# Scans in fewer TensorE batches, 64-row scores of both maps, another pace of the first and last head, and modulation dots held behind a norm

## The chip, the cores and the metric

The kernel runs on one core of a Trainium2 chip. A core has TensorE (matrix products, in the profile PE, its weight loads PEld), VectorE (DVE), ScalarE (ACT), GpSimd (POOL) and SyncE (SP, which here issues the loads and stores). Every engine works through its own queue in order and waits on semaphores that other engines raise. TensorE reads from the on-chip memory and writes into eight accumulator banks of 128 partitions x 512 fp32 values; VectorE and ScalarE read the results from there. The metric is device time of one execution in microseconds (us), as the median of several runs.

## The reference, cut to what matters

One inference step of two layers over 512 latent tokens and 128 context tokens, with width 1024. Layer 0 mixes tokens with a two-directional state-space scan (32 heads in 4 groups, chunks of 128 tokens), layer 1 with differential attention (8 heads, two key maps of width 64 each). Each is followed by a channel mixer. Every sub-layer is normed and modulated by shift, scale and gate, which are products of SiLU(cond) with a weight matrix.

```python
def modulation(cvec, w, b):
    m = jax.nn.silu(cvec) @ w + b
    return jnp.split(m[:, None, :], 6, axis=-1)

def ssd_scan(x, dt, a, bm, cm, h0):               # one direction
    ...
    decay = jnp.exp(jnp.where(tri, seg, -jnp.inf))
    cb = jnp.einsum('bcign,bcjgn->bcijg', cm, bm)
    y_diag = jnp.einsum('bcijge,bcjgep->bcigep', cb[..., None] * decay, xd)
    xw = xd * jnp.exp(a_cs[:, :, -1:] - a_cs)[..., None]
    states = jnp.einsum('bcqgn,bcqgep->bcgepn', bm, xw)
    ...                                            # h_in: states carried from chunk to chunk
    y_off = jnp.einsum('bcqgn,bcgepn->bcqgep', cm, h_in) * jnp.exp(a_cs)[..., None]
    y = (y_diag + y_off).reshape(b, l, nh, p)

def diff_attend(q, k, v, lam):                     # per block of 128 queries
    s = jnp.einsum('bqhcd,bkhcd->bhcqk', qi, k) * DA_SCALE    # c: the two maps
    p = jax.nn.softmax(s, axis=-1)
    w = p[:, :, 0] - lam * p[:, :, 1]
    return jnp.einsum('bhqk,bkhd->bqhd', w.astype(v.dtype), v)
```

Latent queries see 640 keys (512 latent, 128 cached context); context queries see the 128 context keys. The forward and backward scans of a chunk are summed, gated by SiLU(z) and normed by group.

## The kernel before, in words

**Layout.** Activations lie feature-major: 128 features on the partitions, 640 tokens in the free dimension (512 latent, then 128 context). A weight product gives one output tile of 128 features x 640 tokens. Weights arrive as fp32 through SP's queue (`prefetch`, three units ahead, four buffers `raw`) and are split into a high and a low part (`whi` by ScalarE, `wlo` by VectorE, lines 93 and 99 through helpers); activations are split in the same way. A tile is the sum over k of three products, high x high, low x high, high x low, each in two column pieces (256 and 384 columns), so eight k-steps of six matmuls for a width of 1024. All these matmuls are issued at line 102.

**Accumulators.** Three wide buffers of two banks each (`psd`, tag d) serve the weight products and some of the other work; two single banks (`psm`, tags m and y) serve the rest.

**Interleaving.** After each k-step `dense_many` calls `hook` (L74), which advances the generators in the task list; `yield n` asks to be called again n k-steps (ticks) later. So the scans, the attention heads, the norms and the modulation dots run in pieces between the k-steps of weight products. `drain` runs a task to its end at once. The order in the code is not yet the order on the engines: the framework plans each engine's queue ahead of time by its own estimates of durations, takes the earliest instruction in code order that it believes ready, and lets later ready work fill a hole. A tile's buffer must be free before its first writer is planned, so who holds a buffer also sets who can run early.

**Scan** (`ssd_group`, L668, one task per group, while the next tiles x, B, C and z are produced): B and x are transposed chunk by chunk (btp, xtp), the backward states are carried (st: `xw` on VectorE, then a product, then two VectorE steps), and then for every chunk: the product of C and B (cb); for each of two quartets of heads the logarithmic decays of both directions (r, bf16, 96 rows) which ScalarE and VectorE turn into the operands m and qc; four ticks later the quartet's outputs (yp: products of 64 stationary columns into the upper and the lower half of the partitions in turn), added to xf by VectorE; and the next forward state.

**Attention** (`attention`, L1028; `att_head`, L939; `att_tail`, L985): for every head the tiles q, k and v are produced; rotary positions and the split of q and k run on VectorE and ScalarE (`att_q`, `att_k`). For precision the score of a map is made of two products over 128 rows: q's 64 features lie twice, high part on its own half, low part on the other, and k's high part lies on both halves, its low part likewise:

```python
st[m][o] = hi(q); st[m][x] = lo(q)          # o: the map's half, x: the other half
kk = (kh[m] on both halves, kl[m] on both halves)
```

A score tile (sl) takes a wide buffer; VectorE takes the row maximum from it, ScalarE the exponent and the sum, and then it is free. Context scores (sp) are fp32 products over the 64 rows of a map. The tail transposes the weights of all four query blocks, multiplies with v and norms the head. The last head's tail runs under the output projection of the first six heads.

**Norm and modulation.** The weight products that end a sub-layer give the first 256 tokens (half A) and the rest (half B) separately; `norm_task` (L227) norms each half while the next sub-layer's first three tiles run on the other (`start_tiles`, L287). `rms_bcast` sums squares on TensorE (ms), takes the reciprocal root in nine short VectorE steps, and spreads it over the partitions (nbc). `mod_rest` (L478) makes layer 1's modulation on VectorE during ffn0: it loads the conditioning (`cbc`), applies SiLU, and takes 96 dot products (L500) with rows loaded into `mw`; in the code it begins 48 ticks into ffn0, and it is due before ffn0's last weight products.

Of the kernel before, what the change touches and what calls it, by code (L numbers as in the profile page):

```python
# [9 lines left out]
F32 = mybir.dt.float32  # L10
# [8 lines left out]
P = 128  # L19
D = 1024  # L20
# [25 lines left out]
class Step:  # L46


    def __init__(self, ctx, tc, a):
# [7 lines left out]
        self.modtask = None  # L57
        self.down = False
# [168 lines left out]
    def norm_task(self, half, gs, sh, h):  # L227
# [94 lines left out]
    def mod_slots(self, pool, odd, name):  # L322
# [5 lines left out]
        return [xt[:, i, :] for i in range(5)] + [t("qm", 2, i) for i in (5, 6)] + [t("qc0", 1, 7)]  # L328
# [339 lines left out]
    def ssd_group(self, g, xf, Bf, Cf, pool):  # L668

        nc = self.nc  # L670
# [8 lines left out]
        pm = self.psm.tile([P, 512], F32, tag="m", name="btp")  # L679
        for c in range(4):  # L680
            nc.tensor.transpose(pm[:, c * P:(c + 1) * P], Bf[:, c * P:(c + 1) * P], self.ident)
        self.act(bt[:, 0:4, :].rearrange("p c n -> p (c n)"), pm, AF.Copy)
        yield 1
        pm = self.psm.tile([P, 512], F32, tag="m", name="btp")
        nc.tensor.transpose(pm[:, :P], Bf[:, 4 * P:5 * P], self.ident)
        self.act(bt[:, 4, :], pm[:, :P], AF.Copy)
        yield 1
        for c in (3, 2, 1, 4, 0):
            pm = self.psm.tile([P, 512], F32, tag="m", name="xtp")
            for t in range(4):  # L690
                nc.tensor.transpose(pm[:, t * P:(t + 1) * P], xf[t][:, c * P:(c + 1) * P], self.ident)
            self.act(xt[:, c, :], pm, AF.Copy)
            yield 1

        def state(d_, c, out):

            hc = slice(32 * d_ + 8 * g, 32 * d_ + 8 * g + 8)
            xw = sl("xw", "xw", 512, 1)
            v3 = lambda t: t.rearrange("p (h e) -> p h e", h=8)
            self.tt(v3(xw), v3(xt[:, c, :]), self.wst[:, c, hc].unsqueeze(2).to_broadcast([P, 8, 64]), ALU.mult)  # L700
            pm = self.psm.tile([P, 512], F32, tag="m", name="st")
            self.mm(pm, bt[:, c, :], xw, True, True)
            nh = sl("hs", f"h_{d_}_{c}_", 512, 6)
# [4 lines left out]
            self.tt(v3(nh), v3(hs[d_, c]), self.cd[:, c, hc].unsqueeze(2).to_broadcast([P, 8, 64]), ALU.mult)  # L708
# [3 lines left out]
        for c in (3, 2, 1):  # L712
            state(1, c, c - 1)
            yield 2
        for d_ in range(2):
            state(d_, NL, None)
            yield 2

        b4 = lambda ap: ap.unsqueeze(1).to_broadcast([P, 4, P])
        v4 = lambda t: t.rearrange("p (h i) -> p h i", h=4)  # L720
        for c in range(NCH):
            cs = slice(c * P, (c + 1) * P)
            pm = self.psm.tile([P, 512], F32, tag="m", name="cb")
# [5 lines left out]
            for q in range(2):  # L729
                h0 = 8 * g + 4 * q  # L730
                r = self.psd.tile([P, 1024], F32, tag="d", name="r")
                for h in range(4):
                    for d_ in range(2):
                        self.mm(r[:, 512 * d_ + h * P:512 * d_ + (h + 1) * P],
                                self.oh[:, h0 + h:h0 + h + 1].to_broadcast([96, P]), self.R3[d_][:, cs], True, True)
                e = sl("qe", "e", 512, 2)
                m = sl("qm", "m", 512, 2)
                for h in range(4):
                    hh = slice(h * P, (h + 1) * P)
                    self.act(e[:, hh], r[:, hh], AF.Identity, bias=self.C[:, c, h0 + h:h0 + h + 1])  # L740
                    self.act(m[:, hh], r[:, 512 + h * P:512 + (h + 1) * P], AF.Identity,
                             bias=self.C[:, c, 32 + h0 + h:33 + h0 + h])
                self.tt(e, e, m, ALU.min)
                self.act(e, e, AF.Exp)
                for h in range(4):
                    hh = slice(h * P, (h + 1) * P)
                    self.act(m[:, hh], cbb, AF.Copy, scale=self.dt[:, c, 32 + h0 + h:33 + h0 + h])
                    self.stt(m[:, hh], cbf, self.dt[:, c, h0 + h:h0 + h + 1], m[:, hh], ALU.mult, ALU.add)
                self.tt(m, m, e, ALU.mult)
                cs2 = []  # L750
                if c < NL:
                    for d_ in range(2):
                        x = sl(f"qc{d_}", f"qc{d_}", 512, 1)
                        self.act(x, r[:, 512 * d_:512 * d_ + 512], AF.Exp)
                        self.tt(v4(x), v4(x), b4(Cf[:, cs]), ALU.mult)
                        cs2.append(x)
                yield 4
                yp = self.psm.tile([P, 512], F32, tag="y", name="yp")
                for pr in range(2):
                    nt = 1 + len(cs2)  # L760
                    for i in range(nt):
                        for hh in range(2):
# [4 lines left out]
                            self.mm(yp[64 * hh:64 * hh + 64, pr * P:(pr + 1) * P], lhsT, rhs, i == 0, i == nt - 1)  # L767
                for pr in range(2):
                    t = 2 * q + pr
                    self.stt(xf[t][:, cs], xf[t][:, cs], self.svec[:, 4 * g + t:4 * g + t + 1],  # L770
                             yp[:, pr * P:(pr + 1) * P], ALU.mult, ALU.add)
                yield 1
            if c < NL - 1:
                state(0, c, c + 1)
                yield 1
# [98 lines left out]
    def att_v(self, ps, hd, vs, pool):  # L874
# [11 lines left out]
        yield 1  # L886
# [28 lines left out]
    def att_q(self, x, hd, pool):  # L915
# [3 lines left out]
        st = [pool.tile([P, TS], F32R, tag=f"qs{m}", name=f"qs{m}_{hd}", bufs=2) for m in range(2)]  # L919
        for m, (o, x) in enumerate(((slice(0, 64), slice(64, 128)), (slice(64, 128), slice(0, 64)))):  # L920
            self.act(st[m][o], q[o], AF.Copy, scale=DA_SCALE)
            self.stt(st[m][x], q[o], DA_SCALE, st[m][o].bitcast(F32), ALU.mult, ALU.subtract)
        return st

    def att_k(self, x, hd, pool):
# [4 lines left out]
        hi, lo = ([pool.tile([P, T], F32R, tag=f"k{nm}{m}", name=f"k{nm}{m}_{hd}", bufs=1) for m in range(2)]  # L930
                  for nm in "hl")
        for m, (o, x) in enumerate(((slice(0, 64), slice(64, 128)), (slice(64, 128), slice(0, 64)))):
            self.act(hi[m][o], k[o], AF.Copy)
            self.tt(lo[m][o], k[o], hi[m][o].bitcast(F32), ALU.subtract)
            self.act(hi[m][x], hi[m][o].bitcast(F32), AF.Copy)
            self.nc.vector.tensor_copy(lo[m][x], lo[m][o].bitcast(F32))
        return hi, lo

    def att_head(self, hd, qp, kp, qs, k, vs, o, pool):  # L939

        nc = self.nc
# [287 lines left out]
```

## Time and profile before

| what | us |
|---|---|
| median of 3 runs | 1940.85 (1938.77 to 1942.29) |
| the profiled execution: its own time | 1941.6 |
| its span, first to last instruction | 1939.8 |
| TensorE busy in it | 1892.0 |
| VectorE busy in it | 1397.2 |
| ScalarE busy in it | 967.6 |

The span is covered by the stages in this order: first tiles and modulation to about 60 us, the scan layer with its output projection to 604, ffn0 to 1070, attention to 1456, ffn1 to the end. The granted TensorE clock over the span was 0.992.

A line of the timeline has the start and the length in us, the engine, the line, the operation, what it writes and reads, its form (for a matmul rows x stationary columns, then the moving operand), how many were put together, and in brackets the idle time of the engine before it with what ended it. Matmuls are pipelined: a length reaches to the end of the result, so the time that one costs is read from start to start. A line of the chain of waits has start, length, and what the end waited for in that stretch. A line of a list of groups has count, busy us, mean ns, and idle time before with its releaser. Stretches ("windows") list for each engine the busy us and the number of instructions, then the clock and the transfers. ffn1 begins with the same passage as ffn0 but has no modulation dots, so the two can be laid side by side.

### The profile page before, as it was taken

The page shows a single profiled execution, that of the slowest core. Times are in us where ns is not written, and L with a number is a line of the kernel's source. Part 1 is how long each engine was busy: PE and PEld are TensorE (multiplying, and loading weights), DVE is VectorE, ACT ScalarE, POOL GpSimd, SP SyncE. Part 2 cuts the span into 40 slices and gives each one's busy share as a digit, 9 for nine tenths or more (in the row PEclk, how much of TensorE's full clock was granted, in tenths as well). Part 3 has the DMA queues.
Part 4 walks back from the last instruction along what each step waited for, and adds up shares of the span by engine and source line. Part 5 has one row for each costly group of instructions (what it writes and reads, how often), then busy time and mean ns, then how long its engine had stood idle before and what let it go on. Part 6 is the DMA issues. An engine that isn't in the chain of part 4 may idle for free.

```text
span 1939.8 us, 33400 instructions
## 1 busy us (share of the span) xinstructions
PE 1892.0 (98%) x13613; PEld 1785.8 (92%) x13613; DVE 1397.2 (72%) x2681; ACT 967.6 (50%) x1789; POOL 0.2 (0%) x4
## 2 busy tenths in 40 slices
PE   7999999999999999999999999999999999999997
PEld 4888888898988999999999988889899999999997
DVE  4779898888948999984455778888877553553554
ACT  2468585868633542243243576666645441441441
POOL 0000000000000000000000000000000000000000
PEclk8999999999999999999999999999999999999998
DMA  9611212113562456632222211111032222222211
GB/s 336 226 59 58 72 47 71 50 66 92 159 211 75 156 181 198 210 119 73 78 68 84 66 45 49 49 46 40 14 114 88 71 72 77 74 69 87 71 39 55
DMA packets 66729, 184.99 MB, mean 95 GB/s; under 512 B 8336, under 2 KB 14736, under 8 KB 66448
## 3 DMA queue, kind: packets, MB, share of 16 engines
q1 hardware_dynamic: 66000, 182.34, 29.1%
q8 instruction: 107, 1.75, 0.4%
q10 hardware_dynamic: 576, 0.52, 0.1%
q14 instruction: 46, 0.38, 0.1%
HBM read 177.06 MB, written 5.77 MB: 94 GB/s over the span
## 4 chain that ended last, share of the span: by engine, by line
PE 92%; ACT 3%; DVE 2%; DMA 1%; issue 1%; SPq 0%; DVEq 0%; ACTq 0%
PE up L102 30%; PE po L102 24%; PE z L102 6%; PE x L102 5%; PE st L102 4%; PE bc L102 3%; PE yp L102 3%; PE k L102 3%; PE q L102 3%; PE v L102 2%; PE sl L102 2%; PE ov L102 1%; PE modrow L102 1%; PE in L102 1%; PE wt L1007 1%; ACT e L93 1%
## 5 line engine op out<-in xcount | busy, mean ns | idle before, releaser
L93 ACT ACTIVATE whi<-raw 128x1024 fp32r<-128x1024 f32 (+4 forms) x230 | 236.1, 1027 | 410.0 <-PE po L102 232.3
L99 DVE TENSOR_TENSOR wlo<-raw,whi 128x1024 fp32r<-128x1024 f32 (+4 forms) x230 | 270.0, 1175 | 183.6 <-ACT whi L93 182.7
L96 DVE SCALAR_TENSOR_TENSOR xr<-po,mod,xr 128x256 f32<-128x256 f32 (+2 forms) x231 | 89.5, 433 | 162.3 <-PE po L102 162.1
L102 PE MATMUL po<-mh,whi 128*128 128x256 f32 (+1 forms) x704 | 167.6, 310 | 0.0
L102 PE MATMUL po<-ml,whi 128*128 128x256 f32 (+1 forms) x704 | 167.3, 310 | 0.0
L102 PE MATMUL po<-mh,wlo 128*128 128x256 f32 (+1 forms) x704 | 167.1, 309 | 0.0
L102 PE MATMUL up<-h01h,whi 128*128 128x256 f32 (+1 forms) x656 | 149.4, 308 | 0.7 <-ACT uraw L93 0.7
L102 PE MATMUL up<-h01h,wlo 128*128 128x256 f32 (+1 forms) x656 | 149.4, 308 | 0.0
L102 PE MATMUL up<-h11l,whi 128*128 128x256 f32 (+1 forms) x656 | 149.3, 308 | 0.0
L102 PE MATMUL up<-h11h,whi 128*128 128x256 f32 (+1 forms) x656 | 149.3, 308 | 0.0
L102 PE MATMUL up<-h11h,wlo 128*128 128x256 f32 (+1 forms) x656 | 149.3, 309 | 0.0
L102 PE MATMUL up<-h01l,whi 128*128 128x256 f32 (+1 forms) x656 | 149.3, 308 | 0.0
L102 PEld LDWEIGHTS po<-mh,whi 128*128 128x128 f32 x704 | 128.4, 188 | 0.6 <-ACT mh L93 0.4
L102 PEld LDWEIGHTS po<-mh,wlo 128*128 128x128 f32 x704 | 128.6, 188 | 0.0
L102 PEld LDWEIGHTS po<-ml,whi 128*128 128x128 f32 x704 | 128.4, 188 | 0.0
L102 PEld LDWEIGHTS up<-h01h,whi 128*128 128x128 f32 x656 | 119.2, 188 | 1.0 <-ACT uraw L93 1.0
L102 PEld LDWEIGHTS up<-h11h,wlo 128*128 128x128 f32 x656 | 119.3, 188 | 0.0
L102 PEld LDWEIGHTS up<-h11l,whi 128*128 128x128 f32 x656 | 119.3, 188 | 0.0
L102 PEld LDWEIGHTS up<-h01h,wlo 128*128 128x128 f32 x656 | 119.2, 188 | 0.0
L102 PEld LDWEIGHTS up<-h11h,whi 128*128 128x128 f32 x656 | 119.2, 188 | 0.0
L102 PEld LDWEIGHTS up<-h01l,whi 128*128 128x128 f32 x656 | 119.2, 188 | 0.0
L96 DVE SCALAR_TENSOR_TENSOR ca<-uraw,fcw,ca 128x127 f32<-128x127 f32 (+1 forms) x176 | 85.3, 545 | 11.4 <-ACT ca L93 11.4
(498 smaller groups left out, 4509.9 us busy)
## 6 DMA issues: line engine op xcount, KB each, us to landing
raw<-in_w_up SPq DMA_DIRECT2D x88, 512.0 KB, 3.5
mw<-in_modT SPq DMA_DIRECT2D x48, 512.0 KB, 3.6
raw<-in_w_in SPq DMA_DIRECT2D x40, 512.0 KB, 3.5
raw<-in_w_dn SPq DMA_DIRECT2D x32, 448.0 KB, 3.3
raw<-in_w_qkv SPq DMA_DIRECT2D x24, 512.0 KB, 3.5
mr<-in_mod SPq DMA_DIRECT2D x44, 256.0 KB, 5.0
raw<-in_w_so SPq DMA_DIRECT2D x16, 512.0 KB, 4.3
raw<-in_w_dn SPq DMA_DIRECT2D x16, 512.0 KB, 3.7
```

The lines of the kernel that those rows point to most:

```text
L93: return self.nc.scalar.activation(out, in_, func, **k)
L96: return self.nc.vector.scalar_tensor_tensor(out, in0, s, in1, op0, op1)
L99: return self.nc.vector.tensor_tensor(out, a, b, op)
L102: return self.nc.tensor.matmul(out, lhsT, rhs, start=start, stop=stop)
L1007: nc.tensor.transpose(pm[:, b * P:(b + 1) * P], ws[b][:, kc * P:(kc + 1) * P], self.ident)
```

## The change

*Scan.* Transposes go into wide buffers, three batches instead of seven. The backward states and the two context states go in pairs through a wide buffer, and the operand `xw` gets a second buffer. Per chunk, one batch holds the outputs of both quartets of the chunk before it, a forward state and the decays of the first quartet; a second one holds the decays of the second quartet and the next product of C and B. There are six ticks from the second quartet's operands to its outputs; before, there were four. `qc0` and `qc1` get a second buffer.

*Scores.* q and k are split once into a high and a low part without the copies on the other half. The score of a map is the sum of three products over 64 rows, high x high, high x low, low x high; the two maps of a query block take a wide buffer each, and their products are issued in turn, on rows 0 to 63 and 64 to 127. Context scores of both maps share one buffer and one batch. The waits between the blocks are other ones, with their own values for the first head and for the last head and its tail.

*Modulation.* In the second half of ffn0's first norm, the temporaries of the last three feature tiles come from the buffers `mw`, `mw` and `cbc`; so the first loads of `mod_rest` must wait for this norm.

```diff
@@ norm_task
-            t = self.tmp("nt")
+            t = self.tmp("nt") if half != "B" or i < KT - len(self.late) else self.late.pop(0)()
@@ run
+            mw = lambda: pool.tile([P, 1024], F32, tag="mw", name="ntm", bufs=2)
+            self.late = [mw, mw, lambda: pool.tile([P, 2, D], F32, tag="cbc", name="ntc", bufs=1)[:, 0, :]]
@@ ssd_group
-        for c in (3, 2, 1, 4, 0):
-            pm = self.psm.tile([P, 512], F32, tag="m", name="xtp")
...
+        ps = self.dense_ps("xtp")
+        for c in (1, 2):
+            xtr(ps[:, (c - 1) * 512:c * 512], c)
+        self.act(flat(xt[:, 1:3, :]), ps, AF.Copy)
+        yield 2
...
+        for pair in (((1, 3, 2), (1, 2, 1)), ((1, 1, 0), (0, NL, None))):
+            ps = self.dense_ps("st")
+            for i, (d_, c, _) in enumerate(pair):
+                state(d_, c, ps[:, i * 512:(i + 1) * 512])
+            for i, (d_, c, out) in enumerate(pair):
+                carry(d_, c, out, ps[:, i * 512:(i + 1) * 512])
+            yield 3
...
+        def output(c, ops):
+            cs = slice(c * P, (c + 1) * P)
+            yp = self.bank("y", "yp")
+            for q, (m, cs2) in enumerate(ops):
...
+                            o = (2 * q + pr) * P
+                            self.mm(yp[64 * hh:64 * hh + 64, o:o + P], lhsT, rhs, i == 0, i == nt - 1)
+            for t in range(4):
+                self.stt(xf[t][:, cs], xf[t][:, cs], self.svec[:, 4 * g + t:4 * g + t + 1],
+                         yp[:, t * P:(t + 1) * P], ALU.mult, ALU.add)
+        ops = None
+        for c in range(NCH):
+            if ops:
+                output(c - 1, ops)
+            if 0 < c < NL:
+                pm = self.bank("m", "st")
+                state(0, c - 1, pm)
+                carry(0, c - 1, c, pm)
+            ops = [decay(c, 0, *cb)]
+            yield 5
+            ops.append(decay(c, 1, *cb))
+            if c < NL:
+                cb = cbprod(c + 1)
+            yield 6
+        output(NL, ops)
+        yield 1
@@ att_q, att_k
-        st = [pool.tile([P, TS], F32R, tag=f"qs{m}", name=f"qs{m}_{hd}", bufs=2) for m in range(2)]
...
+        hi, lo = (pool.tile([P, TS], F32R, tag=f"q{nm}", name=f"q{nm}_{hd}", bufs=2) for nm in "hl")
+        self.act(hi, q, AF.Copy, scale=DA_SCALE)
+        self.stt(lo, q, DA_SCALE, hi.bitcast(F32), ALU.mult, ALU.subtract)
...
+        hi, lo = (pool.tile([P, T], F32R, tag=f"k{nm}", name=f"k{nm}_{hd}", bufs=2) for nm in "hl")
+        self.act(hi, k, AF.Copy)
+        self.tt(lo, k, hi.bitcast(F32), ALU.subtract)
@@ att_head
-            for m in range(2):
-                r = self.psd.tile([P, 1024], F32, tag="d", name="sl")
-                for j, kk in enumerate((kh, kl)):
...
+            qb = slice(b * P, (b + 1) * P)
+            rs = [self.psd.tile([P, 1024], F32, tag="d", name="sl") for _ in range(2)]
+            for j, (x, kk) in enumerate(((qh, kh), (qh, kl), (ql, kh))):
+                for c0 in (0, 320):
+                    for r, hf in zip(rs, half):
+                        self.mm(r[:, 192 + c0:192 + c0 + 320], x[hf, qb], kk[hf, c0:c0 + 320], j == 0, j == 2)
+            st = stats()
+            em = [softmax(r[:, 192:832], T, m, st) for m, r in enumerate(rs)]
+            yield 2
...
+            if b < 3:
+                yield ((1, 1, 1) if last else (1, 3, 1) if hd else (1, 3, 3))[b]
-        self.tails[hd] = self.add(self.att_tail(hd, w, ws, vs, o, pool), 4)
+        self.tails[hd] = self.add(self.att_tail(hd, w, ws, vs, o, pool), 1 if last else 2)
@@ att_tail, attention
-            yield 2
+            yield 1 if hd == 7 else 2
...
-        bc = yield from self.rms_bcast(lambda: self.wide("obc"), [sq], 0, T, P, 7)
+        bc = yield from self.rms_bcast(lambda: self.wide("obc"), [sq], 0, T, P, 4 if hd == 7 else 7)
...
-            tk.append(self.add(self.att_head(hd, qp, kp, q, k, vs, o, pool), 4))
+            tk.append(self.add(self.att_head(hd, qp, kp, q, k, vs, o, pool), 1 if hd == 7 else 4))
```

More of the change, by code (lines that the diff above doesn't have):

```diff
@@ L57, in __init__ @@
         self.modtask = None
+        self.late = []
         self.down = False
@@ L687, in ssd_group @@
-        yield 1
-        for c in (3, 2, 1, 4, 0):
-            pm = self.psm.tile([P, 512], F32, tag="m", name="xtp")
[L690 to L701, printed above, removed]
+        flat = lambda ap: ap.rearrange("p c n -> p (c n)")
@@ new lines, in ssd_group, with xtr @@
+        tr = lambda out, x, c: nc.tensor.transpose(out, x[:, c * P:(c + 1) * P], self.ident)
+        def xtr(ps, c):
+            for t in range(4):
+                tr(ps[:, t * P:(t + 1) * P], xf[t], c)
+        ps = self.dense_ps("xtp")
+        for c in range(4):
+            tr(ps[:, c * P:(c + 1) * P], Bf, c)
+        xtr(ps[:, 512:], 3)
+        pm = self.bank("m", "btp")
+        tr(pm[:, :P], Bf, 4)
+        self.act(flat(bt[:, 0:4, :]), ps[:, :512], AF.Copy)
+        self.act(xt[:, 3, :], ps[:, 512:], AF.Copy)
@@ L702, in state, with carry @@
+        heads = lambda d_: slice(32 * d_ + 8 * g, 32 * d_ + 8 * g + 8)
+        def state(d_, c, pm):
+            xw = sl("xw", "xw", 512, 2)
+            self.tt(v3(xw), v3(xt[:, c, :]), self.wst[:, c, heads(d_)].unsqueeze(2).to_broadcast([P, 8, 64]), ALU.mult)
             self.mm(pm, bt[:, c, :], xw, True, True)
+        def carry(d_, c, out, pm):
             nh = sl("hs", f"h_{d_}_{c}_", 512, 6)
@@ L707, in state, with cbprod @@
                 return
-            self.tt(v3(nh), v3(hs[d_, c]), self.cd[:, c, hc].unsqueeze(2).to_broadcast([P, 8, 64]), ALU.mult)
+            self.tt(v3(nh), v3(hs[d_, c]), self.cd[:, c, heads(d_)].unsqueeze(2).to_broadcast([P, 8, 64]), ALU.mult)
             self.tt(nh, nh, pm, ALU.add)
             hs[d_, out] = nh
-        for c in (3, 2, 1):
-            state(1, c, c - 1)
-            yield 2
[L715 to L721, printed above, removed]
+        def cbprod(c):
             cs = slice(c * P, (c + 1) * P)
-            pm = self.psm.tile([P, 512], F32, tag="m", name="cb")
+            pm = self.bank("m", "cb")
             self.mm(pm[:, :P], Bf[:, cs], Cf[:, cs], True, True)
@@ new lines, in cbprod @@
+            return cbf, cbb
+        for pair in (((1, 3, 2), (1, 2, 1)), ((1, 1, 0), (0, NL, None))):
[6 more added lines that the diff above has]
+        pm = self.bank("m", "st")
+        state(1, NL, pm)
+        carry(1, NL, None, pm)
+        cb = cbprod(0)
@@ L941, in att_head @@
         nc = self.nc
-        kh, kl = k
+        (qh, ql), (kh, kl) = qs, k
+        half = [slice(64 * m, 64 * m + 64) for m in range(2)]
         def softmax(s, n, m, st):
@@ L957, in combine @@
             self.stt(w, e0[:, :n], st[:, 4:5], e1[:, :n], ALU.mult, ALU.add)
-        em, st = [], stats()
-        for m in range(2):
-            r = self.psd.tile([P, 1024], F32, tag="d", name="sp")
-            ms = slice(64 * m, 64 * m + 64)
-            self.mm(r[:, :TP], qp[ms], kp[ms], True, True)
-            em.append(softmax(r[:, :TP], TP, m, st))
-            yield 1
+        r = self.psd.tile([P, 1024], F32, tag="d", name="sp")
+        for m, hf in enumerate(half):
+            self.mm(r[:, 512 * m:512 * m + TP], qp[hf], kp[hf], True, True)
@@ L967, in att_head @@
+        st = stats()
+        em = [softmax(r[:, 512 * m:512 * m + TP], TP, m, st) for m in range(2)]
+        yield 2
+        last = hd == 7
         w = pool.tile([P, TP], F32, tag="wp", name="wp", bufs=1)
         combine(w, TP, *em, st)
+        yield 3 if last else 4
         ws = []
         for b in range(4):
[L971 to L979 removed]
```

115 lines of the change are left out of this document (48 added, 67 removed).

## The prediction

> **What bounds the kernel now.** I read the page first, then the chain of waits, then TensorE's timeline in one stretch of each stage that the change touches.
>
> ```profile
> span 1939.8 us, 33400 instructions
> PE 1892.0 (98%) x13613; PEld 1785.8 (92%) x13613; DVE 1397.2 (72%) x2681; ACT 967.6 (50%) x1789; POOL 0.2 (0%) x4
> ...
> PE 92%; ACT 3%; DVE 2%; DMA 1%; issue 1%; SPq 0%; DVEq 0%; ACTq 0%
> ```
>
> TensorE sets the end: 92% of the chain is its own work. So an edit is worth what it takes out of TensorE's stream: columns, the price of changing the form of a matmul, and waits that stop its one queue. Work saved on VectorE or ScalarE counts only where TensorE waits for it.
>
> The price of a change of form shows where the scan's output products (yp, 64 stationary columns, two column halves in turn) stand between weight products.
>
> ```profile
> 240.17 0.46 PE L102 MATMUL x<-h00h,whi 128*128 128x256 f32 x2
> 240.56 0.44 PE L102 MATMUL yp<-m,xt 128*64 128x128 f32 x4
> 240.83 0.61 PE L102 MATMUL yp<-qc,h 128*64 128x128 f32 x8
> 241.27 0.39 PE L102 MATMUL yp<-m,xt 128*64 128x128 f32 x4
> ...
> 242.02 0.56 PE L102 MATMUL x<-h00l,whi 128*128 128x256 f32 x2
> 242.42 0.46 PE L102 MATMUL x<-h00h,wlo 128*128 128x256 f32 x2
> ...
> 228.53 0.46 PE L102 MATMUL x<-h00l,whi 128*128 128x256 f32 x2
> 228.82 1.02 PE L102 MATMUL st<-xw,bt 128*128 128x512 f32 x2
> 229.28 0.85 PE L102 MATMUL x<-h00h,wlo 128*128 128x256 f32 x2
> 229.97 0.62 PE L102 MATMUL r<-R,oh 96*128 96x128 bf16 x8
> ...
> 230.78 0.45 PE L102 MATMUL x<-h00l,whi 128*128 128x256 f32 x2
> ```
>
> The timeline gives starts; a weight pair (256 and 384 columns) undisturbed takes 0.29 us (228.53 to 228.82). From 240.17 to 242.42 lie two pairs and 24 yp: 2.25 - 0.58 = 1.67 us. Eight yp take 0.44 (240.83 to 241.27), so 24 take 1.32, and **0.35 us is the price of entering and leaving the form**. The full-height fp32 product st has none: 228.82 to 229.97 holds one pair and two passes, 1.15 - 0.29 = 0.86 for 1024 columns, and inside yp the rate is the same 0.85 ns a column for two halves at once. The bf16 batch r: 230.78 - 229.97 - 0.29 = 0.52, some 0.07 above its stream.
>
> **The change, part by part.**
>
> *Scan.* All products stay (three transposed pieces share a wide buffer, states go in pairs, both head quartets of a chunk put their outputs together). Transposes and states have st's full-height form, so putting them together saves 0 on TensorE. The yp batches are what counts; below, their row in the view of the tile yp, and xw's in the list of groups.
>
> ```profile
> L102 PE MATMUL yp<-m,xt x320: 272/273/325, 133.4 to 515.7; 128*64 128x128 f32 x160
> ```
>
> ```profile
> L99 DVE TENSOR_TENSOR xw<-xt,wst 128x512 f32<-128x512 f32 x32 | 21.9, 683 | 1.3 <-PE st L102 1.3
> ```
>
> By the code there are 4 groups x 5 chunks x 2 quartets = 40 batches; counted in the timeline between these first and last starts they stand in 56 unbroken runs, as the planner slid weight products into some. After, the code has 20; I estimate that one in four is still broken, 25 runs. (56 - 25) x 0.35 = -10.8 us. Ends: no run broken, 36 x 0.35 = -12.6; if all but the merging of whole batches stays as now, 40 left, 16 x 0.35 = -5.6. Half of the 40 r batches now stand beside yp: -20 x 0.07 = -1.4, or 0. Against it: in one tick TensorE now meets outputs, a state and r, and the state's xw multiply stands on VectorE behind four xf updates that wait for those outputs. If the planner does not fill that hole with weight products, xw's 0.68 us and about half as much (an estimate) for the last update before it stop TensorE at 12 places: +12. xw reads nothing of the outputs, so it can run ahead; I take +1. Behind a waiting state stand r and then all later weight products. **Scan: -11, from -14 to +3.**
>
> *Scores.*
>
> ```profile
> 1236.21 0.46 PE L102 MATMUL sl<-kh,qs 128*128 128x320 f32 x2
> 1236.51 0.45 PE L102 MATMUL sl<-kl,qs 128*128 128x320 f32 x2
> 1236.80 0.46 PE L102 MATMUL q<-h10l,whi 128*128 128x256 f32 x2
> ...
> 1237.38 1.25 PE L102 MATMUL obc<-rs_y,cst 128*128 128x160 f32 x8
> 1238.36 0.56 PE L102 MATMUL q<-h10h,whi 128*128 128x256 f32 x2
> ...
> 1254.95 0.45 PE L102 MATMUL v<-h10h,wlo 128*128 128x256 f32 x2
> 1255.33 0.48 PE L102 MATMUL sp<-kp,qp 64*128 64x128 f32 x2
> 1255.75 0.56 PE L102 MATMUL v<-h10h,whi 128*128 128x256 f32 x2
> 1256.15 0.46 PE L102 MATMUL v<-h10l,whi 128*128 128x256 f32 x2
> ...
> 1262.38 0.48 PE L102 MATMUL ms<-osq,cst 128*32 128x160 f32 x8
> 1262.79 0.56 PE L102 MATMUL sl<-kh,qs 128*128 128x320 f32 x2
> 1264.71 0.56 PE L102 MATMUL q<-h10h,whi 128*128 128x256 f32 x2 [1.07 <-ACT e L93]
> ```
>
> Now a query block has 2 maps x 4 products of 320 columns at 0.147 us (four in 0.59, 1236.21 to 1236.80), with no change of form: 1.18 us. After, it has 12 products of 64 rows, the maps in turn on rows 0-63 and 64-127. This is a form of its own; its price is read from sp, the one 64-row product in the trace: 1256.15 - 1254.95 - 0.58 = 0.62, less two passes of 128 columns at 0.85 ns (0.22), is 0.40. Whether two row halves run side by side no row shows. The nearest is column parts: eight obc passes of 160 columns take 0.98 us in turn, eight ms passes of the same width on four column parts 0.41 with the price of the form in it. I take side by side: 6 x 0.147 + 0.40 = 1.28 us, +0.10 a block, x 32 = +3.4. The other end is one after the other: 12 x 0.147 + 0.40 = 2.16, +0.98, x 32 = +31.5. Between them lies a bound by the weight loads, each product loading its own.
>
> ```profile
> 594.12 1.10 PE L102 MATMUL nbc<-rs_y,cst 128*128 128x64 f32 x8
> 595.04 0.42 PE L102 MATMUL po<-y15l,whi 128*128 128x384 f32 x1
> ...
> 1143.46 0.56 PE L102 MATMUL sl<-kh,qs 128*128 128x320 f32 x2 [2.11 <-ACT e L93]
> ...
> 1427.27 0.36 PE L102 MATMUL po<-o0h,whi 128*128 128x256 f32 x1 [0.87 <-DVE xr L96]
> ```
>
> Eight 64-column passes take 0.92, 0.115 each where 64 columns would be 0.055: a load of 128 columns can't come faster. If the two halves' loads queue, a pair costs 0.23: 6 x 0.23 + 0.40 = 1.78, +0.60 a block, +19.
>
> [...]
>
> The context scores sp go from two batches a head to one: -0.40, and -0.22 if the maps overlap: 8 x 0.62 = -4.9 (or -3.2).
>
> Waits: at the step from v to q TensorE stands 1.07 us for a score buffer that ScalarE's exponent still reads (row 1264.71), at five like places, 1189 to 1338. The new pace puts score blocks at ticks 2 and 5 of q and of k, away from that step: -5.3. But a block now takes two of the three wide buffers at once, while the weight product holds the third; I give back half, 2.7. First head: waits like 2.11 go with the wider pace, -2. Last head: its tail ends some 8 ticks earlier under the output projection, so waits like 0.87 shrink, -2.
>
> The lighter q and k preparation on VectorE and ScalarE is off the path: 0. **Attention: 3.4 - 4.9 - 2.6 - 4 = -8, from -16 to +25.**
>
> *Modulation dots behind the norm.*
>
> ```profile
> 595.23 8.75 PE po L102 x50
> ...
> 635.26 0.86 PE up L102 x4
> ...
> 1444.88 8.73 PE po L102 x50
> ...
> 1477.13 0.90 PE up L102 x6
> ```
>
> ```profile
> 612.63 1.22 DVE L500 CUSTOM_DVE_ANT_0 junk<-mw,cbc 128x1024 bf16<-128x1024 f32 x1
> ...
> 616.80 1.61 PE L102 MATMUL nbc<-rs_y,cst 128*128 128x96 f32 x8 [2.87 <-DVE rs_y L96]
> ...
> 846.78 1.22 DVE L500 CUSTOM_DVE_ANT_0 mw<-mw,cbc 128x1024 f32<-128x1024 f32 x1
> ```
>
> The chain has the same passage twice: from the last po run to the first up run 40.03 us before ffn0, with the dots, and 32.25 before ffn1, without: 7.8 us. In the first, 1.22 us dots stand on VectorE between the short steps of the second half's reciprocal root, and TensorE waits 2.87 us for it. The norm's last three temporaries now take the buffers cbc and mw, so the conditioning load, its silu and the first dots can't start until the norm has read them. The dots are over at 848, 180 us before they are due, so their delay costs nothing. SP's queue is passed too: weight loads behind the held cbc and mw loads wait, but three units are loaded ahead at some 7 us a unit. What can be late is ScalarE: two tanh passes of some 1.06 us now fall where the first up tiles are copied out. I take 7.8 - 0.8 = **-7, from -8.5 to -4.**
>
> **Sum.** -11 - 8 - 7 = -26. The profiled execution took 1941.6 us (span 1939.8 and 1.8 around it), 0.75 above the median 1940.85. 1941.6 - 26 = 1915.6; as a median 1914.9, say **1915**.
>
> **Rivals.**
> 1. *Row halves one after the other.* For it: no row shows them together. Against: column parts do. Scores +31.5, context scores -3.2, last and first head -4, no wait regained: +24.3; with -18 from the rest +6.3, **1947, slower**. It decides once a block costs over 1.18 + 25.2 / 32 = 1.97 us (25.2: the 18, 3.2 and 4 on the other side).
> 2. *Weight loads of the halves queue*: +19 instead of +3.4, **1930**. The row 594.12 speaks for it.
> 3. *The planner breaks the scan's batches up again, or the state waits for its xw*: scan -1, **1925**. The 16 extra runs now speak for it; the longer lead (6 ticks, not 4) against.
> 4. *Buffers.* Two of three wide buffers in one block, so TensorE waits 1.07 us, as at 1264.71, at two steps of each head more: 16 x 1.07 = 17, and nothing regained, 2.6: **1935**. [...]
> 5. *The hold does not hold*, dots run as before: **1922**.
>
> **Chances.** Forecast 0.48, rival 1 0.15, 2 0.11, 3 0.11, 4 0.09, 5 0.06. 0.2% of 1940.85 is 3.9 us, about what a measurement of this kernel can tell from no change. Slower is 0.12 of rival 1; no difference are its other 0.03 and 0.05 of rivals 2 and 4; the rest is faster: 0.80, 0.08, 0.12. Range: below, the gains at their ends (-14, -16, -8.5) don't all come, 1900; above up to rival 4 and part of rival 1, 1942. The likeliest case alone: 1905 to 1924.
>
> **What would show it.** Right: yp in about 25 runs, each with 0.35 us; sl starts in pairs a few ns apart and a block of 1.28 us; one sp batch a head; no dot between 604 and 630 and a passage of 32 to 33 us; no 1.07 us wait at v to q. Wrong: sl starts 0.15 us apart; yp runs still over 40; new waits for ACT e inside q or k; a late copy-out of the first up tiles.

## The result, and the profile after

The changed kernel took 1923.19 us (median of 4 runs, 1921.78 to 1923.86), the kernel before 1941.57 beside it (4 runs, 1938.77 to 1943.18). The ratio is 0.9906 with a 95% interval from 0.9889 to 0.9923: 18.2 us faster, where 26 had been forecast. One of the runs of the scan part alone, further down, took 2300.53 us at a granted clock of 0.753 and is left out of its median and ratio. First the head of the page after, and its chain's shares:

```profile
span 1920.0 us, 33586 instructions
PE 1887.8 (98%) x13741; PEld 1781.4 (93%) x13741; DVE 1377.3 (72%) x2649; ACT 944.5 (49%) x1753; POOL 0.2 (0%) x4
...
PE 94%; DVE 2%; DMA 1%; ACT 1%; issue 0%; SPq 0%; DVEq 0%; ACTq 0%
```

TensorE still sets the end, now with 94% of the chain and not 92%. Its busy time fell by only 4 us while the span fell by 20: at this level the gain looks like waits removed. The stages say more. The table has the length of each stage of the two profiled executions, cut at the start of the first product of a stage, and beside it, in brackets, what the granted clock took of it: the sum, over stretches of 1 us, of length times (1 - granted clock).

| stage | before | after | difference |
|---|---|---|---|
| to the first scan tile x | 58.2 (5.1) | 56.7 (1.7) | -1.5 |
| scan, to the output projection's first product | 402.8 (0) | 396.0 (0) | -6.8 |
| output projection and passage, to ffn0's first up product | 174.3 (3.4) | 165.9 (0) | -8.4 |
| ffn0, to the first q product | 469.8 (0) | 470.7 (0) | +0.9 |
| attention, to ffn1's first up product | 371.9 (1.7) | 368.5 (5.1) | -3.4 |
| ffn1, to the end | 462.8 (5.9) | 462.2 (5.9) | -0.6 |

The 5.9 of the last row is a drop that starts 12 us ahead of the end, where TensorE is busy for 1.6 us only, so it costs little. The first row is not the change's: over the thirteen profiles of this study it goes from 55.5 to 59.2 us with nothing edited there. The other rows repeat to some 0.1 us where the code of a stage is the same (scan: 402.5, 402.8 and 402.8 in three kernels with the old one, 395.8 to 396.0 in seven with the new one; ffn0, the clock aside, and ffn1 to 1.5 us). So stages are compared below by their lengths in the traces, and whole kernels by medians.

**The passage.** The chain of waits of the changed kernel, the rows that answer to 595.23, 635.26, 1444.88 and 1477.13 before:

```profile
586.42 8.75 PE po L103 x50
...
618.71 105.62 PE up L103 x720
1425.66 8.73 PE po L103 x50
...
1457.92 105.62 PE up L103 x720
```

Ahead of ffn0 it takes 32.29 us now, ahead of ffn1 32.26: the dots are out of it (the first one in ffn0 starts at 631.71). What the old passage had lost is seen in the view of stretches of the kernel before (busy us and number of instructions of PE, PEld, DVE, ACT, POOL, then the granted clock and the transfers); the edges were put where the clock changes:

```profile
613.81:617.22 3.41, 0.55 (x6) 0.45 (x5) 3.41 (x10) 0.00 (x0) 0.00 (x0) 1.00 0.55 186
617.22:620.63 3.41, 2.00 (x10) 1.76 (x9) 2.76 (x9) 1.29 (x4) 0.00 (x0) 0.50 0.66 221
```

TensorE is busy for 0.55 of 3.41 us, and then has half the clock for two such stretches (617.2 to 624.0). That costs 3.4 us; the wait of 2.87 us quoted in the prediction was less than half of the loss.

**The scan.** Timelines of the two kernels at the ends of the stage, before first, and in the changed kernel around one chunk's outputs, with VectorE's row that ends the second quartet's operand:

```profile
58.19 0.45 PE L102 MATMUL x<-h00h,whi 128*128 128x256 f32 x2
...
460.98 0.46 PE L102 MATMUL po<-y0h,whi 128*128 128x256 f32 x2
```

```profile
56.69 0.46 PE L103 MATMUL x<-h00h,whi 128*128 128x256 f32 x2
...
250.84 0.44 PE L103 MATMUL yp<-m,xt 128*64 128x128 f32 x4
...
255.03 0.44 PE L103 MATMUL yp<-m,xt 128*64 128x128 f32 x4
...
452.65 0.54 PE L103 MATMUL po<-y0h,whi 128*128 128x256 f32 x2
```

```profile
253.86 0.69 DVE L100 TENSOR_TENSOR m<-m,e 128x512 f32<-128x512 f32 x1
```

The stage went from 402.79 to 395.96 us. The two quartets of a chunk are one batch in the code, but stand 4.2 us apart in the queue: the second one's operand is finished at 254.55, and the planner filled the hole with weight products. The yp runs, counted as for the prediction, fell from 56 to 42, the r runs from 49 to 43.

**The scores.** A block in the changed kernel with both wide buffers free, and one in the k tile of a later head; beside it ScalarE in the same time:

```profile
1142.66 0.46 PE L103 MATMUL k<-h10h,wlo 128*128 128x256 f32 x2
1143.05 0.56 PE L103 MATMUL sl<-kh,qh 64*128 64x320 f32 x4
...
1144.12 0.56 PE L103 MATMUL k<-h10h,whi 128*128 128x256 f32 x2
1144.52 0.46 PE L103 MATMUL k<-h10l,whi 128*128 128x256 f32 x2
...
1179.03 0.46 PE L103 MATMUL k<-h10h,wlo 128*128 128x256 f32 x2
1179.42 0.56 PE L103 MATMUL sl<-kh,qh 64*128 64x320 f32 x2
...
1179.94 0.41 PE L103 MATMUL sl<-kh,qh 64*128 64x320 f32 x1
...
1181.41 0.45 PE L103 MATMUL k<-h10l,whi 128*128 128x256 f32 x2
```

```profile
1177.45 1.06 ACT L94 ACTIVATE whi<-raw 128x1024 fp32r<-128x1024 f32 x1 [0.65 <-PE q L103]
...
1179.14 0.58 ACT L94 ACTIVATE q<-q 128x512 f32<-128x512 f32 x1
1179.62 0.27 ACT L94 ACTIVATE qp<-q 128x128 f32<-128x128 f32 x1
```

In the first, the products of the two maps start in pairs a few ns apart, and the block costs 1144.52 - 1142.66 - 0.58 = 1.28 us. In the second only the first map starts at 1179.42; the other follows at 1179.94, after ScalarE has copied out q (until 1179.89), whose wide buffer it takes, and the block costs 1181.41 - 1179.03 - 0.58 = 1.80 us. The fourth block of a head is like it (1.90, the exponent being the late reader: in the same head ScalarE's pass ends at 1184.34, and the second map starts at 1184.49). No engine is shown idle in this: for those 0.52 us TensorE has products of one map only, on half of its rows.

The view of waits of TensorE over the attention stage, before and then after (total us, times, longest):

```profile
PE sl L102 <- ACT e L93: 6.6, 7, 2.1
PE q L102 <- ACT e L93: 5.6, 6, 1.1
```

```profile
PE po L103 <- ACT e L94: 1.5, 2, 1.2
...
PE sl L103 <- ACT e L94: 0.6, 1, 0.6
```

With the smaller rows left out here the sums are 15.9 and 4.1: the listed waits shrank by 11.8 us, the 1.07 us ones all gone, but the stage by 3.4 only. Part of the rest is in the clock. Stretches of the changed kernel, in the first head and in the last:

```profile
1109.38:1112.79 3.41, 2.75 (x17) 2.10 (x16) 3.41 (x5) 3.25 (x7) 0.00 (x0) 1.00 0.08 22
1112.79:1116.20 3.41, 3.41 (x15) 3.08 (x14) 3.01 (x8) 2.78 (x7) 0.00 (x0) 0.50 0.00 0
...
1361.98:1365.39 3.41, 1.61 (x9) 1.15 (x8) 2.90 (x7) 3.07 (x8) 0.00 (x0) 1.00 0.00 0
1365.39:1368.80 3.41, 3.41 (x22) 2.31 (x23) 2.13 (x7) 0.83 (x1) 0.00 (x0) 0.50 0.21 62
```

The second drop lasts until 1372.2. Together they take 5.1 us, against 1.7 us for one drop in the attention before. The clock aside, attention went from 370.2 to 363.4, -6.8 us.

Where in the stage that lies is seen when it is cut at the first products of the q tiles (head 0's tiles come before the stage). The clock's part is in brackets again; e6 is an experiment further down.

| attention | before | after | e6 |
|---|---|---|---|
| heads 1 and 2 | 85.0 (1.7) | 75.4 (1.7) | 69.6 (0) |
| heads 3 to 6 | 149.4 (0) | 145.7 (0) | 146.2 (0) |
| head 7 and the output projection | 137.6 (0) | 147.3 (3.4) | 141.6 (0) |

So a middle head gained 0.9 us, though two of its four blocks cost 1.80 and 1.90 us. The two ends moved by 9.5 and 9.8 us in opposite directions. Part of that is work that now runs later: 12 score products of 128 rows or their like, 6 products with v (ov) and 4 transposes went from the first stretch to the last, some 3.6 us (an estimate, at 0.147, 0.24 and 0.11 us each).

### The profile page after: what moved, and what is told of

It reads as the page before. It is cut to its first block, busy times and chain, and to the rows that moved or that the text cites. A ratio compares the mean times of both kernels' runs of the same rounds, so it can differ in the third digit from the quotient of the medians.

```text
span 1920.0 us, 33586 instructions
## 1 busy us (share of the span) xinstructions
PE 1887.8 (98%) x13741; PEld 1781.4 (93%) x13741; DVE 1377.3 (72%) x2649; ACT 944.5 (49%) x1753; POOL 0.2 (0%) x4
## 4 chain that ended last, share of the span: by engine, by line
PE 94%; DVE 2%; DMA 1%; ACT 1%; issue 0%; SPq 0%; DVEq 0%; ACTq 0%
PE up L103 30%; PE po L103 25%; PE z L103 6%; PE x L103 5%; PE st L103 5%; PE bc L103 3%; PE yp L103 3%; PE v L103 3%; PE q L103 2%; PE sl L103 2%; PE k L103 2%; PE ov L103 1%; PE modrow L103 1%; PE r L103 1%; PE wt L1052 1%; PE in L103 1%
## 5 line engine op out<-in xcount | busy, mean ns | idle before, releaser
L103 PE MATMUL up<-h01h,wlo 128*128 128x256 f32 (+1 forms) x656 | 149.4, 308 | 0.0
L103 PE MATMUL up<-h11h,wlo 128*128 128x256 f32 (+1 forms) x656 | 149.4, 308 | 0.0
L97 DVE SCALAR_TENSOR_TENSOR ca<-uraw,fcw,ca 128x511 f32<-128x511 f32 (+1 forms) x176 | 85.2, 546 | 11.7 <-ACT ca L94 11.7
```

The source lines that it names most:

```text
L97: return self.nc.vector.scalar_tensor_tensor(out, in0, s, in1, op0, op1)
L103: return self.nc.tensor.matmul(out, lhsT, rhs, start=start, stop=stop)
```

## The experiments

### One part alone, three times

e1 is the kernel before with `late` in `norm_task` and `run` only; e2 with `ssd_group` and the second buffer of qc0 only; e3 with `att_q`, `att_k`, `att_head`, `att_tail` and the pauses of attention only.

> The kernel before with the modulation hold alone (three norm tiles of the B half taken from the row buffers); scan and attention untouched. Theory (the passage from the output projection into the first feed-forward shrank from 40.03 to 32.29 us because of the hold and of nothing else): 7.7 us shorter, about 1934, passage 32 to 33 us, no modulation dot ahead of the last norm row. Rival (part of the 7.7 us came from the scan, which left the vector engine less behind at the projection): 3 to 5 us shorter, passage 35 to 37.

> The kernel before with the scan part alone (doubled tiles, pairs of states, both quartets of a chunk put out together, second buffers); hold and attention as before. Theory (the scan part is worth what the two traces differ by up to the end of the output projection, and does not lean on the other two): 8.8 us shorter, about 1932.5, yp runs 42 as in the changed kernel. Rival (each batch saved pays 0.35 us and nothing else, so the 14 fewer yp runs and 6 fewer r runs are all of it): 5 to 6 us shorter, about 1936.

> The kernel before with the attention part alone (64-row scores of both maps in one batch, other pace, first and last head); hold and scan as before. Theory (waits of 11 us and form changes of 3 us saved, but blocks that cost 1.78 us where 1.18 were paid, and a last head that gives 8 us back): 2.7 us shorter, about 1938.5, score blocks 1.7 to 1.9 us on the mean. Rival (attention gains its 10.7 us and the last head's loss comes from the hold or from the feed-forward's late dots): 8 to 11 us shorter, about 1931.

| part | median | ratio, 95% interval | us of 1940.5 |
|---|---|---|---|
| hold | 1932.94 | 0.9963 (0.9949 to 0.9976) | -7.2 |
| scan | 1933.16 | 0.9958 (0.9944 to 0.9973) | -8.2 |
| scores | 1937.32 | 0.9980 (0.9971 to 0.9990) | -3.9 |

The last column is worked out from the ratios. Its sum is -19.3, within the interval of the whole change (-14.9 to -21.5): the parts add, and each lies nearer to its theory than to its rival (e1's interval just reaches the rival's 3 to 5, and e2's holds the rival's 5 to 6 as well). In the traces each stage repeats what the whole change shows. The passage of e1, by its chain of waits, is 624.84 - 592.55 = 32.29:

```profile
592.55 8.75 PE po L103 x50
...
624.84 105.62 PE up L103 x720
```

and e1 has no drop of the clock there, while e2 and e3, without the hold, have the same 3.4 us as before. The hold is worth 7.9 us by that stage (174.28 to 166.37), of which 3.4 is clock. The scan of e2, by its timeline, takes 451.76 - 55.90 = 395.86, and the projection behind it 0.6 us less (173.67):

```profile
55.90 0.46 PE L102 MATMUL x<-h00h,whi 128*128 128x256 f32 x2
...
451.76 0.54 PE L102 MATMUL po<-y0h,whi 128*128 128x256 f32 x2
```

So the scan alone is worth 7.5 us by these two stages; in the whole change it is 7.3 (6.8, and 0.5 by which the passage is shorter than e1's). e3's attention takes 368.5 us with 5.1 of clock, to 0.1 us what the changed kernel has.

### Maps one after the other in the queue

```diff
-            for j, (x, kk) in enumerate(((qh, kh), (qh, kl), (ql, kh))):
-                for c0 in (0, 320):
-                    for r, hf in zip(rs, half):
+            for r, hf in zip(rs, half):
+                for j, (x, kk) in enumerate(((qh, kh), (qh, kl), (ql, kh))):
+                    for c0 in (0, 320):
```

> The changed kernel with the twelve products of a block issued map by map (six on the upper rows, then six on the lower) and not in turn; same operands, same buffers, same pace. Theory (two row halves work at once only when their products stand in turn in the queue): a block with both buffers free goes from 1.27 us to about 2.1 (twice six products of 0.143 and the price of form 0.40), 32 blocks, so 12 to 26 us longer than the changed kernel, 1935 to 1949; blocks that wait for the second buffer lose less, as their first map then works meanwhile. Rival (side by side by the engine itself, whatever the order, or the wait for the second buffer is all that counts): within 3 us of the changed kernel, 1920 to 1926.

It took 1925.36 us, 2 more than the changed kernel: in the total the rival's number. Its timeline at a block:

```profile
1220.27 0.46 PE L103 MATMUL k<-h10h,wlo 128*128 128x256 f32 x2
1220.65 0.55 PE L103 MATMUL sl<-kh,qh 64*128 64x320 f32 x2
1221.05 0.30 PE L103 MATMUL sl<-kl,qh 64*128 64x320 f32 x1
1221.05 0.41 PE L103 MATMUL sl<-kh,qh 64*128 64x320 f32 x1
...
1222.54 0.45 PE L103 MATMUL k<-h10l,whi 128*128 128x256 f32 x2
```

The block costs 1222.54 - 1220.27 - 0.58 = 1.69, not 2.1 and not 1.28, and so do the blocks of the middle heads (1.54 to 1.69). The second map's first product is the seventh in the queue, and starts with the third one: the halves overlap even in this order, only 0.40 us late. So turns are worth 0.41 us to a block with free buffers and nothing to one whose second buffer is late anyway (1.80 and 1.90 against 1.69). Both theories were half right. The middle heads' period rose from 36.45 to 37.66 us, of which the four blocks explain some 0.5, and attention, the clock aside, from 363.4 to 369.2; the total hides most of that because the last head's drop of the clock (3.4 us) did not come in this execution.

### The late buffer first

```diff
-                    for r, hf in zip(rs, half):
+                    for r, hf in reversed(list(zip(rs, half))):
```

> The changed kernel with the two maps' products exchanged within each pair: the second map, whose wide buffer comes free last, is first in the queue. Nothing else differs. Theory (blocks of the k tile cost 1.78 to 1.93 us because the engine stands for the second wide buffer, and the first map's product that runs meanwhile is worth little): the same within 2 us, 1921 to 1925, and the stand shows as idle time ahead of the block in place of a long block. Rival (what costs is that a product that starts alone breaks the pairing for the rest of the block): blocks fall to 1.3 us, 8 to 12 us shorter, 1911 to 1915.

It took 1936.74 us, 13.5 more, which neither theory expected. It is not a clean test, since the planner put other work around the blocks. At the third block of a head, ScalarE now copies q out ahead of the cast of weights and not behind it; its rows, and TensorE's:

```profile
1181.25 0.60 ACT L94 ACTIVATE q<-q 128x512 f32<-128x512 f32 x1
...
1181.88 1.07 ACT L94 ACTIVATE whi<-raw 128x1024 fp32r<-128x1024 f32 x1
```

```profile
1182.43 0.46 PE L103 MATMUL k<-h10h,wlo 128*128 128x256 f32 x2
1182.81 0.57 PE L103 MATMUL sl<-kh,qh 64*128 64x320 f32 x4
...
1184.29 0.46 PE L103 MATMUL k<-h10l,whi 128*128 128x256 f32 x2
```

The same block costs 1.28 here: with the copy early, the 0.52 us were gone. That bears out the cause of the 1.80, though the exchange of the maps came with it. The fourth block, which now waits with its first product, went from 1.90 to 2.56, so the first map's lone work was worth something. The middle heads are 0.2 us longer; the loss lies in the first and the last head, where TensorE stands idle for 11.9 of the stage's 13.8 us, and 10.2 us of clock went there in place of 5.1.

### The old 128-row products at the new pace

The operands and products of the kernel before (eight products of 128 rows a block), two wide buffers and all pauses as in the changed kernel (`att_k` as before too):

```diff
-        hi, lo = (pool.tile([P, TS], F32R, tag=f"q{nm}", name=f"q{nm}_{hd}", bufs=2) for nm in "hl")
+        st = [pool.tile([P, TS], F32R, tag=f"qs{m}", name=f"qs{m}_{hd}", bufs=2) for m in range(2)]
...
+            for m, r in enumerate(rs):
+                for j, kk in enumerate((kh, kl)):
+                    for c0 in (0, 320):
+                        self.mm(r[:, 192 + c0:192 + c0 + 320], qs[m][:, qb], kk[m][:, c0:c0 + 320], j == 0, j == 1)
```

> The changed kernel with the scores' operands and products of the kernel before (128 rows, high and low half stacked, eight products a block and not twelve), but still both maps in one batch, with two buffers and the pace of the changed kernel. Theory (the price of the 64-row form, 0.40 us a block, and the first map's lone start are what the blocks lose): blocks of 1.2 us on the mean, 32 x (1.78 - 1.2) = 18 us shorter at most, less the six copies more a head on the scalar and vector engines, which may bring waits back: 1905 to 1915. Rival (the wait for the second buffer is the whole loss and stays, and the copies delay the rotary embedding): 1920 to 1928.

It took 1913.02 us (ratio to before 0.9855, 0.9840 to 0.9869), 10 less than the changed kernel: the theory's range. The timeline at a block, and a stretch of the first head:

```profile
1215.28 0.45 PE L103 MATMUL k<-h10h,wlo 128*128 128x256 f32 x2
...
1217.04 0.46 PE L103 MATMUL k<-h10l,whi 128*128 128x256 f32 x2
```

```profile
1110.93:1114.34 3.41, 1.66 (x12) 1.38 (x10) 3.37 (x7) 3.37 (x8) 0.00 (x0) 1.00 0.08 22
```

A block costs 1217.04 - 1215.28 - 0.58 = 1.18, and its products cost no more where it is broken (0.87 and 0.30 us at 1164.81 and 1165.92). A late second buffer hardly occurs here: ScalarE's copy of q ends at 1214.61, ahead of the block, and at the fourth block (1219.39) the exponent ends at 1219.43, while the first map's products run. Attention takes 357.3 us, and no drop of the clock is in it, though TensorE stands for 1.76 us in that stretch. So 11.2 us went: 5.1 of clock and 6.1 of blocks and waits. By the table of heads none of this lies in heads 3 to 6 (146.2 us, and 145.7 in the changed kernel), although two of the four blocks of a head cost 1.18 there in place of 1.80 and 1.90; the gain is at the two ends. So the price of the form and the lone start, from which the range was worked out, are not shown to be what the total fell by. The copies of q and k that came back stand on VectorE and ScalarE, and no row of TensorE's waits names them; what takes the blocks' gain back in the middle heads is open.

### A longer lead in the scan

`yield 5` and `yield 6` of a chunk became `yield 3` and `yield 8`.

> The changed kernel with the scan's two pauses a chunk 3 and 8 ticks and not 5 and 6, so that the second quartet's decay has 8 ticks before its product is due. Theory (the batches of yp broke in two because the second quartet's operand came about 4 us after the batch was due; a longer lead mends part of them): yp runs 42 to about 35, each 0.35 us, 2.5 us shorter, about 1920.7. Rival (the first quartet's decay is now the late one, or the buffers of r bind): the same or up to 3 us longer.

It took 1919.90 us (0.9890, 0.9875 to 0.9904; it overlaps the changed kernel's 0.9889 to 0.9923). The yp runs fell to 35 as expected. By the timeline the stage takes 453.12 - 58.15 = 394.97, 1.0 less, and the projection 0.6 less:

```profile
58.15 0.46 PE L103 MATMUL x<-h00h,whi 128*128 128x256 f32 x2
...
453.12 0.46 PE L103 MATMUL po<-y0h,whi 128*128 128x256 f32 x2
```

So the trace shows 1.6 us, against 7 x 0.35 = 2.5; that the gain is the 3.3 of the medians isn't shown.

### The pace of the last and of the first head

e8 undoes the last head's own pauses (`last = False`, and head 7's numbers in `att_tail` and `attention` as for the others); e11 gives the first head the pauses of the middle ones:

```diff
-                yield ((1, 1, 1) if last else (1, 3, 1) if hd else (1, 3, 3))[b]
+                yield ((1, 1, 1) if last else (1, 3, 1))[b]
```

> The changed kernel with the last head at the pace of the others (the shorter pauses and earlier starts of head 7 undone). Theory (the last head gives back 8 us because its blocks are called faster than their buffers come free, so they break in pieces): up to 5 us shorter, 1918 to 1922. Rival (without the faster pace the second feed-forward waits longer for the tail of the last head): 4 to 10 us longer, 1927 to 1933.

> The changed kernel with the first head at the pace of the middle heads (pauses 1, 3, 1 and not 1, 3, 3). Theory (the first head's third and fourth block cost 2.47 and 3.45 us because no other work of attention is ready and the wide buffers are short, whatever the pause): within 1.5 us of the changed kernel, 1922 to 1925. Rival (the longer pause is what keeps the first head from a stall): 3 us longer or more.

e8 took 1922.81 us, e11 1921.00 (0.9900, 0.9884 to 0.9917): neither can be told from the changed kernel, though e11's median lies just below the expected 1922. In e8 the last head's blocks are whole and cost 1.27, and attention without the clock still takes 363.4 us, as in the changed kernel. In e11 it takes 364.1, and the first head's drop of the clock is gone. e8 lies just above its theory's 1918 to 1922. In this kernel these paces are worth nothing that the runs can show, but for where the clock falls.

### Both edits that gained

e9 has the edits of e6 and e7, e10 those of e8 as well.

> The changed kernel with both edits that were faster alone: the scores' 128-row operands and products of the kernel before (10 us shorter alone) and the scan's pauses of 3 and 8 ticks (3.3 us shorter alone). Theory (the two act in different stages and add): 1909 to 1911. Rival (the scan's gain was a shift of when work is called, which the attention takes back): 1912 to 1914.

> The kernel of e9 with the last head at the pace of the others. Theory (the last head's faster pace is worth nothing: alone it measured 1922.8 against 1923.2): within 2 us of e9. Rival (with 128-row blocks, which lose nothing when broken, the faster pace pays): 3 to 6 us longer than e9.

e9 took 1909.45 us, 0.9843 of before (0.9828 to 0.9857), and beats both kernels, the changed one by some 14 us. The median is that of gains that add; its interval overlaps e6's, but in its trace the scan and the stage behind it have e7's lengths (395.08 and 165.31) and attention has e6's (357.3). e10 took 1916.05 (0.9873, 0.9859 to 0.9888), 6.6 longer, just above the rival's 3 to 6; but 3.4 of the 5.2 us that its attention is longer (362.5 against 357.3) are a drop of the clock from 1388.6 to 1395.5 that e9 does not have.

## Why the prediction was right, and where not

| term | forecast | by the traces |
|---|---|---|
| scan | -11 | -7.3 |
| attention | -8 | -3.4 |
| hold | -7 | -7.9 |
| sum | -26 | -18.6 |

The sign, the range and the hold were right; the two larger terms were mis-sized: the number of yp runs in the scan, and the blocks whose second buffer is late in the attention. The range, 1900 to 1942, held even an unchanged kernel, so the time's lying in it proves little; of its ends, +3 for the scan and -16 for attention are not added up in the prediction.

*Scan.* The estimate "one in four is still broken, 25 runs" failed: 42 runs, the prediction's own sign of being wrong ("yp runs still over 40") and the first half of rival 3, though not at its price. The 14 runs fewer give 14 x 0.35 = 4.9 and the r runs some 0.4; 2.0 us of the 7.3 are left, of which 0.4 is idle time: TensorE stood for 2.0 us in the scan before and 1.6 after. The rest I can't put to a row. So the cost of +1 for the state's wait did not come. What the step missed is that the lead of the second quartet, 6 ticks, had to cover VectorE and ScalarE work that ended some 4 us late; e7 shows that the lead sets part of the number of runs (42 to 35).

*Scores.* The block of 1.28 us, argued from column parts, measured 1.28 where both buffers were free, so rivals 1 and 2 fall. It failed as a figure for all 32 blocks: two of four in a middle head cost 1.80 and 1.90. Rival 4 had the right place (two of the three wide buffers, two steps a head) but not the shape: 0.5 to 0.6 us each and not 1.07, as half-used TensorE time and not as idle time. The context scores, from each start to the next, fell from 6.64 to 3.37 us, -3.3 and not -4.9: the other end that was named.

*Waits.* I gave half of the 5.3 us back and took 4 for the first and last head, 6.6 in all; the listed waits shrank by 11.8. With 3.3 of sp and the clock's +3.4 that would leave -11.7; the stage gained 3.4, so by difference the blocks and what is broken around them cost 8.3 more than before, not 3.4. Most of that is not in the middle heads: their stretch gained 3.6 us, where 4.3 of idle time and 1.6 of context scores went, so 2.3 came back there. Some 4.5 lie in head 7 and the output projection, where idle time (4.7 to 3.3 us), context scores (-0.4), the moved work (3.6, the estimate above) and the clock (3.4) account for the rest of the 9.8; 1.5 is left for heads 1 and 2. The -2 for each end head was put down to their paces, which e8 and e11 show to be worth nothing; the waits of heads 1 and 2 did go (idle time 7.0 to 1.0 us), but which part of the new order of the blocks did that, no run separates.

*Clock.* It is missing from the sum. It made 3.4 of the hold's 7.9, which the comparison of two passages held without my naming it: there the number was right for a reason that the prediction did not give. And it took 3.4 from attention; leaving it out, attention gained 6.8 against 8. That the two just cancel is luck.

*Hold.* Rival 5 falls (first dot at 631.71). The 0.8 set aside for late copy-outs was not needed; ffn0 is 0.1 us longer in e1.

## What to carry to other kernels

Where an operand needs two buffers at once, the second one's release is the due time: here a wait of TensorE turned into half-used time (0.5 to 0.6 us a block) that no view lists as idle, so cost a stage from start to start, in a middle step and at the ends, and remember that work which moves from one end to the other looks like a gain and a loss. Time a packed form against the unpacked one: here a block was 1.28 us with the two maps in turn in the queue and starting together, 1.69 with the maps apart in the queue and 1.80 to 1.90 with one buffer late, and 1.18 unpacked. The kernel with the unpacked form was 10 us better, though about half of that was clock and the rest did not lie in the middle heads. Look at the granted clock around every wait that an edit makes or removes, because a short wait can cost more after it than in it: here one of 2.87 us was followed by a drop that cost 3.4.

## What the runs showed of the hardware

**The clock.** In the traces of the two kernels the drops ahead of the last one of each span are to 0.50 and last 3.41 us or a multiple of it (before 10.24, 6.83 and 3.41 us, after 3.41, 3.41 and 6.83), at 1.7 us a piece. They start on steps of 3.413 us: in the kernel before at 23.30, 617.22, 1118.98 and 1927.94 us, which is 174, 147 and 237 times 3.413 us apart. The drop at 617.22 followed a stretch in which TensorE was busy for 0.55 of 3.41 us; the one of the changed kernel at 1112.79 followed one with 2.75, mostly with half-height products of one map. The busy time of that stretch alone does not decide. Two stretches that begin and end on these steps, of the kernel before (just ahead of its drop at 1118.98) and of e10 (82 steps ahead of its drop at 1388.63):

```profile
1115.57:1118.98 3.41, 2.10 (x11) 1.60 (x12) 2.80 (x7) 2.84 (x9) 0.00 (x0) 1.00 0.18 71
```

```profile
1108.73:1112.15 3.42, 1.65 (x12) 1.38 (x11) 3.38 (x7) 3.38 (x8) 0.00 (x0) 1.00 0.07 22
```

The first, with 2.10 us busy, was followed by half the clock, the second, with 1.65, was not; both hold products of 128 rows. The stretch of e6 shown above lies off the steps: counted back from its drop at 1901.66, the stretches on them there are 1109.76 to 1113.18 and 1113.18 to 1116.59, busy for 2.83 and 2.25 us, and neither was followed by a drop. What decides stays open.

The executions of one kernel did not all drop their clock alike: the four of e8 took 1918.79, 1920.92, 1924.70 and 1925.13 us at a mean granted clock of 0.996, 0.995, 0.991 and 0.991. So a clock's part that is read from one trace holds for that execution. In the profiles of e3 and of the changed kernel the drops of attention take the same 5.1 us.

**Row halves.** In the block of 1.28 us two halves of 64 rows run side by side: four products, two of each map, take 0.30 us from start to start (1143.44 to 1143.74), as long as two of one map alone (0.29, 1110.69 to 1110.98). The twelve in turn would be 12 x 0.147 = 1.76, and the 1.28 has the 0.40 for the form in it. In e4's block TensorE did not start its products in the order of its queue: the first one of the lower half started at 1221.05, ahead of three products of the upper half that stood before it.
